# Reordering the loads, stores and modulation work of the first stage of a two-layer backbone (one core, fp32 in three products)

## The chip, the cores and the metric

The kernel runs on one core of one Trainium2 chip. The metric is the device time of one execution in microseconds (us). The kernel before takes 1304.21 us, the median of three runs (1303.91 to 1308.95). The engines are named as in the profile: PE multiplies matrices, DVE is the vector engine, ACT the scalar engine, POOL the third elementwise engine, and SP issues the DMA transfers of nearly all loads and stores. Each engine works through its own instructions in order.

## The reference, cut to what matters

Two layers act on a stream `x` of 1024 tokens with 1024 channels; 256 context tokens feed the first layer only. Each layer is modulated by a conditioning vector, and one layer's result is gated by it:

```python
shift, scale, gate = jnp.split(sc @ mod_w[l] + mod_b[l], 3, axis=-1)   # sc = silu(c); scc = silu(c_ctx) likewise
hx = modulate(rmsnorm(x, norm_g[l]), shift, scale)
hc = modulate(rmsnorm(ctx, norm_g[l]), shift_c, scale_c)               # first layer only
# first layer: va, vg, ga, xb, gb = split(h @ w_in)
#   y_a = silu(layernorm(depthwise_conv31(va * sigmoid(vg)))) * silu(ga)
#   y_b = bidirectional gated recurrence over depthwise_conv4(xb) * silu(gb); its initial states come from hc
#   out = concat(y_a, y_b) @ w_out
# second layer: u, g = split(h @ w_in); d = multi-scale pooling of u;
#   out = ((d, in 4 groups, @ w_grp) * scale * silu(g)) @ w_out
x = x + gate * out
```
The result is a final rmsnorm of `x`.

## The kernel before

**Precision.** Every fp32 operand of a large product is split in two halves, hi and lo: ACT casts the fp32 tile to hi (`wh_...`), then DVE or POOL subtracts to make lo (`wl_...`). A product is three matmuls: hi by hi, hi by lo, lo by hi. So a weight tile passes four stations before PE can use all of it: its load, the cast on ACT, the subtraction, and the PE's turn. PE can begin with hi alone; the third matmul of a triple is the first that needs lo. `wload` (L117) does load and split in one call; the engine that subtracts is an argument.

**Queues.** `load` (L107 to L115) issues a transfer on SP and ties it behind the previous one made by `load`, so that these transfers are issued in the order in which the program names them, until the first stage ends with `chain[0] = None`. SP also waits, at a transfer, for whatever the transfer needs (a store for the copy that makes its tile, a load for the last reader of its buffer), and everything behind it waits too. Elsewhere a planner orders instructions on each engine from the program's order and its own estimates of readiness.

**Folding.** The second layer's grouped product with `w_grp` is folded into a part of its input weights ahead of time (`fold`, L238 to L268). For one group, two 512 KB tiles of the group's matrix (`graw`) are loaded and split to `gh`, `gl`. Then come four steps; each loads one 512 KB weight tile `wu` and runs two sets of 12 matmuls. ACT copies each set's result to a tile `fo` (six buffers, `fpool`), and SP stores it to a DRAM buffer `wfold`, 256 KB each. The folding of two groups (16 stores) is spread over the first stage, where PE would otherwise have little to do; the buffer is read back only in the second layer, from about 795 us on. The other two groups are folded later and store from ACT's queue.

**The first stage** (L279 to L435, to about 78 us) interleaves four streams, in an order written out by hand in L396 to L435: the folding; the eight tiles of `x` (`x_load`, with squares on ACT and their sums on DVE); the first layer's modulation (`mod_loads`, `mod_cols`, in four blocks b of 512 KB x 4 loads `modw`: 16 narrow matmuls `modr` a load in groups, a copy `modrow` on ACT, then eight matmuls `modt`); and at last `modulate`, which makes the eight split tiles of the modulated stream, `h0h`, `h0l`. `rstd_cols` (L197) turns the sums of squares into the scale of each token with small matmuls (`ms_x`). At the start, before anything else on PE, two matmuls spread the conditioning vector over the partitions (`c`, L378) and ACT applies silu to it into `cL`. A short series on ACT and DVE works out the decay rates of the recurrence from `lam` (L171 to L185); it needs other ACT tables (exp) than silu.

**The context** (L383 to L394): two tiles `cx` of the context are loaded, squared, scaled by the reciprocal norm (`ctx_scale`), modulated (`modulate_ctx`) and split to `cth` (ACT) and `ctl` (DVE).

**The first products** (L672 on). PE runs `xb` (the 48 matmuls of the first recurrence input, with a small `ms_c` between them), `xbc` (24 matmuls of the same weight on the context), then the loop over eight channel blocks j: `vg` (48), `va` (48), the next block's `xbc` (24), and 12 triples of gate matmuls `g`, mixed with the next `xb`. ACT and DVE turn `xb` and `xbc` into `uc` (the short convolution), `uh` and `ul`, on which the gates depend; DVE makes `u` from `va` and the sigmoid `sg`. The weight of vg is loaded by `wload` at L678 with POOL subtracting, that of `va` by `raw_load` and `raw_split`, also with POOL. In the pass j = 0, DVE also works out the first layer's gate (L711 to L718): for each of eight blocks a 512 KB tile `modT` is loaded into a tile `L`, and one instruction multiplies it by `cL` and sums each row (a "dot" in what follows); these dots stand on DVE ahead of `u`.

After this come the conv branch's DVE work spread as "fill" steps over the loop, the output product of the first layer, and the second layer.

## Time and profile before

| | |
|---|---|
| median of 3 runs | 1304.21 us (1303.91 to 1308.95) |
| the profiled execution's own time | 1306.04 us |
| its span, first to last instruction | 1304.0 us |
| mean granted clock of PE | 0.993 |
| loaded and stored | 181.81 MB, mean 139 GB/s |

The profile comes from one execution. Its page gives busy times for each engine, and a chain of work that ended last: followed back from the last instruction, at each step to what released it. A row of the chain has the start, the length, then engine, tile and source line. A row of the timeline has start and length, engine, line, operation, the tile written and those read, partitions x elements, and in brackets how long the engine idled before and what ended that. A row of a table of windows names its columns in its head.

All that the diff touches lies in the first 120 us. There the trace shows: start to about 10 us, first loads, spreads of c, decay rates; 10 to 78 us, the first stage proper, with the DMA engines nearly full in its first two thirds; 78 to 89 us, `xb`; 89 to 98 us, part of `vg` and `xbc`; 98 to 120 us, the rest of `vg`, `va` and `xbc`, with the gate's dots on DVE; from 137 us on the loop's passes, 42.48 us each.

### The profile page before, as it was taken

The numbers are of one execution on the slowest core, as the hardware profiler recorded it, in microseconds if no ns is written. First come the engines' busy times: TensorE is split into PE (matmuls) and PEld (weight loads), VectorE is DVE, ScalarE is ACT, GpSimd is POOL, SyncE is SP. The second block draws the span as 40 slices with busy tenths as digits, with TensorE's granted clock in tenths as the row PEclk, the third lists the DMA queues.
The fourth block names the chain that finished last, engine by engine and source line by source line (L and its number), as shares of the span: only waits on it lengthen the run. The fifth ranks groups of instructions, "written<-read, shape, count | busy, mean of one in ns | idle before, by whom it ended". The sixth has DMA issues, their size and how long they took to land.

```text
span 1304.0 us, 16066 instructions
## 1 busy us (share of the span) xinstructions
PE 1267.2 (97%) x5780; PEld 1036.4 (79%) x5780; DVE 1132.8 (87%) x1756; ACT 646.1 (50%) x935; POOL 300.2 (23%) x151
## 2 busy tenths in 40 slices
PE   7999999999999999999999999999999999999995
PEld 5687888888888887888887778788888888788784
DVE  6669999999999999978968959999999987977776
ACT  7443666566566633236535346634343434645442
POOL 0212644364535546543210022000000000000002
PEclk9999999999999999999999999999999999999997
DMA  9953111122011233442418566334333334868623
GB/s 360 337 178 112 57 42 64 52 62 69 37 57 57 81 127 124 154 145 89 147 47 287 181 195 178 106 121 154 121 126 101 121 113 137 309 217 281 214 85 129
DMA packets 82865, 181.81 MB, mean 139 GB/s; under 512 B 7777, under 2 KB 27617, under 8 KB 82786
## 3 DMA queue, kind: packets, MB, share of 16 engines
q1 hardware_dynamic: 74338, 176.60, 39.9%
q10 hardware_dynamic: 8448, 4.20, 1.1%
q8 instruction: 45, 0.74, 0.2%
q14 instruction: 34, 0.28, 0.1%
HBM read 136.72 MB, written 44.04 MB: 139 GB/s over the span
## 4 chain that ended last, share of the span: by engine, by line
PE 55%; DVE 29%; DMA 8%; issue 3%; ACT 3%; POOL 1%; SPq 0%; POOLq 0%; ACTq 0%; DVEq 0%
DVE conv L444 7%; PE wob L444 6%; PE vg L444 5%; PE va L444 4%; PE xb L444 4%; DVE l L444 4%; PE g L444 3%; DMA yr_t<-y_t 2%; PE fold L262 2%; PE fold L260 2%; PE fold L261 2%; PE ga L135 2%; PE ga L444 2%; PE ga L134 2%; PE ga L136 2%
## 5 line engine op out<-in xcount | busy, mean ns | idle before, releaser
L444 DVE SCALAR_TENSOR_TENSOR conv<-u,sm,conv 128x505 f32<-128x505 f32 (+6 forms) x224 | 153.5, 745 | 1.0
L1588 POOL TENSOR_TENSOR o<-x,rr 128x256 f32<-128x256 f32 (+1 forms) x9 | 8.0, 925 | 452.6 <-ACT rr L1576 449.6
L444 ACT ACTIVATE l<-g,sm 128x512 f32<-128x512 f32 (+1 forms) x96 | 58.7, 618 | 60.0 <-PE g L444 59.2
L104 POOL TENSOR_TENSOR wl_wu<-wr_wu,wh_wu 128x1024 fp32r<-128x1024 f32 x12 | 28.7, 2390 | 171.5 <-ACT wh_wu L103 128.1
L260 PE MATMUL fold<-gh,wh_wu 128*128 128x512 f32 x128 | 53.2, 416 | 4.9 <-ACT wh_wu L103 4.9
L444 POOL TENSOR_TENSOR l<-l,l 128x1280 f32<-128x1280 f32 x16 | 47.1, 2965 | 25.6 <-ACT l L444 15.1
L444 PE MATMUL wob<-ybl,wh_wob 128*128 128x512 f32 x128 | 50.1, 392 | 2.3 <-POOL ybl L444 2.3
L261 PE MATMUL fold<-gl,wh_wu 128*128 128x512 f32 x128 | 51.7, 404 | 0.0
L262 PE MATMUL fold<-gh,wl_wu 128*128 128x512 f32 x128 | 50.3, 405 | 0.3 <-POOL wl_wu L104 0.3
L444 PE MATMUL gb<-h0h,wl_gb 128*128 128x512 f32 x128 | 49.9, 390 | 0.2 <-POOL wl_gb L444 0.2
L444 PE MATMUL gb<-h0l,wh_gb 128*128 128x512 f32 x128 | 49.8, 389 | 0.0
L444 PE MATMUL wob<-ybh,wh_wob 128*128 128x512 f32 x128 | 49.8, 389 | 0.0
L444 PE MATMUL gb<-h0h,wh_gb 128*128 128x512 f32 x128 | 49.8, 389 | 0.0
L444 PE MATMUL vg<-h0h,wh_vg 128*128 128x512 f32 x128 | 49.8, 389 | 0.0
L444 PE MATMUL vg<-h0l,wh_vg 128*128 128x512 f32 x128 | 49.8, 389 | 0.0
L444 PE MATMUL wob<-ybh,wl_wob 128*128 128x512 f32 x128 | 49.8, 389 | 0.0
L444 PE MATMUL vg<-h0h,wl_vg 128*128 128x512 f32 x128 | 49.8, 389 | 0.0
L444 PE MATMUL va<-h0h,wh_va 128*128 128x512 f32 x128 | 49.8, 389 | 0.0
L444 PE MATMUL va<-h0l,wh_va 128*128 128x512 f32 x128 | 49.8, 389 | 0.0
L444 PE MATMUL va<-h0h,wl_va 128*128 128x512 f32 x128 | 49.8, 389 | 0.0
L444 DVE TENSOR_TENSOR_SCAN l<-l,l 128x256 f32<-128x256 f32 (+1 forms) x32 | 48.7, 1521 | 1.1
L103 ACT CAST wq_g<-wr_g 128x512 fp32r<-128x512 f32 x48 | 28.2, 620 | 40.9 <-DVE wr_g L887 12.9
(593 smaller groups left out, 4291.4 us busy)
## 6 DMA issues: line engine op xcount, KB each, us to landing
wr_wu<-wu SPq DMA_DIRECT2D x16, 512.0 KB, 4.5
modw<-modW SPq DMA_DIRECT2D x16, 512.0 KB, 7.1
x_part<-xp SPq DMA_DIRECT2D x32, 256.0 KB, 2.4
mod<-modT SPq DMA_DIRECT2D x32, 256.0 KB, 3.7
wr_v<-wfold SPq DMA_DIRECT2D x16, 512.0 KB, 3.6
wr_g<-wg SPq DMA_DIRECT2D x16, 512.0 KB, 4.4
wr_wo<-wo SPq DMA_DIRECT2D x16, 512.0 KB, 4.6
yr_t<-y_t SPq DMA_DIRECT2D x16, 512.0 KB, 5.9
```

The costliest lines, as they stand in the source:

```text
L103: return (nc.scalar.copy(hi, src), eng.tensor_tensor(out=lo, in0=src, in1=hi.bitcast(F32), op=sub))
L104: eng.tensor_tensor(out=lo, in0=src, in1=hi.bitcast(F32), op=sub))
L134: nc.tensor.matmul(ps, hi[:, kc], xh[k][:, cols], start=(k == 0), stop=False)
L135: nc.tensor.matmul(ps, hi[:, kc], xl[k][:, cols], start=False, stop=False)
L136: nc.tensor.matmul(ps, lo[:, kc], xh[k][:, cols], start=False, stop=(k == ks - 1))
L260: nc.tensor.matmul(ps, wh[:, kc], gh[i], start=(i == 0), stop=False)
L261: nc.tensor.matmul(ps, wh[:, kc], gl[i], start=False, stop=False)
L262: nc.tensor.matmul(ps, wl[:, kc], gh[i], start=False, stop=(i == 3))
L444: last[eng] = f(*args, **kw)
L1588: nc.gpsimd.tensor_tensor(out=o[:, k - k0], in0=v, in1=rr, op=mult)
```

## The change

Nothing that is computed changes; where and when it is done does:

- The small tables `sm` and `eg` are loaded inside the chain, `sm` behind the second x tile and `eg` as the last of the chain. `ccol` follows `sm`, `ident` comes later. Ahead of everything now go half of group 0's matrix, the first fold weight `wu_0`, and the other half.
- The decay rates become a function that the program calls after the second block's `mod_cols`. In the planner's order its ACT instructions (Abs, exp) now stand among the squares of the first x tiles, on both sides of the silu of `cpad`.
- The stores of the first two groups' folds are collected and issued on SP behind the context's loads: six, then the load of vg's weight, then ten. The pool of `fo` tiles grows from six to eleven. In SP's order the load of va's weight stands behind the twelfth store, and the last four stores right ahead of the gate's loads.
- Ten matmuls of 128 columns on a constant tile stand at PE's start (`warm`); their result isn't used.
- The spreads of c (`spread_c`) move to before the last fold step, and use `cL` itself as the landing tile.
- The gate's loads and dots (`gates`) move from the loop's first pass to the end of the first stage, into tiles of `xpool`, as do the context's tiles `cx`. In DVE's order, dot 16 now stands behind the reciprocal of the context's norm, dot 17 between the scaling of the context and the modulation of its first half, 18 between the halves, 19 to 21 behind the second, 22 and 23 behind `ctl`.
- The weight of vg is loaded and split in the first stage, by DVE instead of POOL.
- On PE the order after `xb` becomes one matmul of `xbc`, 37 of `vg`, 23 of `xbc`, 11 of `vg`, then `va`; it was 1, 24, 23, 24. From the gate matmuls of the first pass on, the order on all engines is as before.

```diff
@@ -104,14 +104,14 @@
                 eng.tensor_tensor(out=lo, in0=src, in1=hi.bitcast(F32), op=sub))
 
 
-    chain = [None]
+    chain, chained = [None], [True]
 
     def load(out, src):
         with ExitStack() as lctx:
-            if chain[0] is not None:
+            if chained[0] and chain[0] is not None:
                 lctx.enter_context(tc.issue_after(chain[0].ins))
             d = nc.sync.dma_start(out, src)
-            if chain[0] is not None:
+            if chained[0]:
                 chain[0] = d
 
     def wload(src, name, eng, n=D, out=None):
@@ -142,9 +142,7 @@
 
 
     sm = base.tile([P, N_SM], F32, name="sm")
-    nc.sync.dma_start(sm, small)
     eg = base.tile([P, 4 * 16], F32, name="eg")
-    nc.sync.dma_start(eg, edge)
 
     def col(o, n=1):
         return sm[:, o : o + n]
@@ -168,21 +166,23 @@
     sa = base.tile([P, NL], F32, name="sa")
     sb = base.tile([P, NL], F32, name="sb")
     sz = base.tile([P, NL], F32, name="sz")
-    nc.scalar.activation(sa, lam, AF.Abs)
-    nc.scalar.activation(sa, sa, AF.Exp, scale=-1.0)
-    nc.vector.tensor_scalar(out=sb, in0=sa, scalar1=2.0, scalar2=None, op0=add)
...
-    nc.vector.tensor_scalar(out=cneg, in0=sa, scalar1=-8.0, scalar2=None, op0=mult)
+
+    def decay_rates():
+        nc.scalar.activation(sa, lam, AF.Abs)
+        nc.scalar.activation(sa, sa, AF.Exp, scale=-1.0)
+        nc.vector.tensor_scalar(out=sb, in0=sa, scalar1=2.0, scalar2=None, op0=add)
...
+        nc.vector.tensor_scalar(out=cneg, in0=sa, scalar1=-8.0, scalar2=None, op0=mult)
 
 
     def rstd(acc, eps, name, wn=0):
@@ -237,8 +237,10 @@
 
     def fold(g, raw_tile, out_tile, g_tile=None, w_tile=None):
         g_tile = g_tile or dtile
-        gh, gl = [], []
+        gh, gl, early = [], [], None
         for i in range(2):
+            if g == 0 and i == 1:
+                early = wload(wu[g, 0], f"wu_{g}_0", nc.vector)
             raw = raw_tile(f"graw_{g}_{i}")
             load(raw, grp[g, i])
             th = g_tile(f"gh_{g}_{i}", F32R)
@@ -251,8 +253,12 @@
             ws = [wload(wu[g, kp], f"wu_{g}_{kp}", nc.gpsimd, out=w_tile[kp]) for kp in range(KT // 2)]
             yield
         for kp in range(KT // 2):
-            wh, wl = (wload(wu[g, kp], f"wu_{g}_{kp}", nc.vector if g == 0 else nc.gpsimd)
-                      if w_tile is None else ws[kp])
+            if kp == 0 and early is not None:
+                wh, wl = early
+            elif w_tile is None:
+                wh, wl = wload(wu[g, kp], f"wu_{g}_{kp}", nc.vector if g == 0 else nc.gpsimd)
+            else:
+                wh, wl = ws[kp]
             for s in range(2):
                 ps = psum(f"fold_{g}_{kp}_{s}")
                 for i in range(4):
@@ -263,13 +269,22 @@
                 dst = wfold[g][:, :, 2 * kp : 2 * kp + 2, :]
                 o = out_tile(f"fo_{g}_{kp}_{s}")
                 nc.scalar.copy(o, ps)
-                (nc.sync if g < 2 else nc.scalar).dma_start(dst[:, :, s, :].rearrange("m p c -> p m c"),
-                                    o.rearrange("p (m c) -> p m c", c=P))
+                dst, o = dst[:, :, s, :].rearrange("m p c -> p m c"), o.rearrange("p (m c) -> p m c", c=P)
+                if g < 2:
+                    stores.append((dst, o))
+                else:
+                    nc.scalar.dma_start(dst, o)
             yield
 
 
     EVAC = 1000
 
+    stores = []
+
+    def store_folds(n):
+        while n and stores:
+            load(*stores.pop(0))
+            n -= 1
 
     cpool = tc.alloc_tile_pool(name="cpool", bufs=1)
     cth = [cpool.tile([P, D], F32R, name=f"cth{i}") for i in range(2)]
@@ -277,7 +292,7 @@
     cL = cpool.tile([P, D], F32, name="cL")
     hh, hl, ch, cl = [], [], [], []
     with ExitStack() as sctx:
-        fpool = sctx.enter_context(tc.tile_pool(name="fpool", bufs=6))
+        fpool = sctx.enter_context(tc.tile_pool(name="fpool", bufs=11))
         gpool = sctx.enter_context(tc.tile_pool(name="gpool", bufs=6))
         spool = sctx.enter_context(tc.tile_pool(name="spool", bufs=1))
 
@@ -293,7 +308,7 @@
             for _ in range(n):
                 next(folds, None)
 
-        cx = [spool.tile([P, D], F32, name=f"cx_{i}") for i in range(2)]
+        cx = []
 
 
         xs = []
@@ -369,16 +384,29 @@
             for h in range(2):
                 sumsq(acc[h], t[:, HALF[h]], H, k == 0, f"xsq_{k}_{h}")
 
-        chain[0] = nc.sync.dma_start(ccv, ccol)
-        nc.scalar.activation(cpad[:, :, 0:2], ccv, AF.Silu)
-        load(cx[0][:1], cc[0:1])
-        load(idx, ident)
-        ps = banks("c_0", 0)
-        for h in range(2):
-            nc.tensor.matmul(ps[h], ones[:1], cx[0][:1, HALF[h]], start=True, stop=True)
-        for h in range(2):
-            nc.scalar.activation(cL[:, HALF[h]], ps[h], AF.Silu, scale=float(D))
+        warm = psum("warm")
+        for i in range(10):
+            nc.tensor.matmul(warm[:, :P], ones, ones, start=True, stop=True)
+
+        def spread_c():
+            load(cL[:1], cc[0:1])
+            ps = banks("c_0", 0)
+            for h in range(2):
+                nc.tensor.matmul(ps[h], ones[:1], cL[:1, HALF[h]], start=True, stop=True)
+            for h in range(2):
+                nc.scalar.activation(cL[:, HALF[h]], ps[h], AF.Silu, scale=float(D))
+
+        def gates():
+            for m in range(2 * KT, 3 * KT):
+                raw = xtile(f"mod0_{m}")
+                load(raw, modT[0, m])
+                nc.vector.scalar_tensor_tensor(out=raw, in0=raw, scalar=1.0, in1=cL, op0=mult, op1=mult,
+                                               accum_out=m0[:, 0, m : m + 1])
+            nc.vector.tensor_tensor(out=m0[:, 0, 2 * KT :], in0=m0[:, 0, 2 * KT :],
+                                    in1=col(O_MB + 2 * KT, KT), op=add)
+
         def ctx_load(i):
+            cx.append(xtile(f"cx_{i}"))
             load(cx[i].rearrange("p (k n) -> p k n", n=C), ctxT[4 * i : 4 * i + 4].rearrange("k p n -> p k n"))
             for q4 in range(4):
                 sumsq(accc, cx[i][:, q4 * C : (q4 + 1) * C], C, i + q4 == 0, f"csq_{i}_{q4}")
@@ -394,22 +422,28 @@
                 modulate_ctx(k)
 
         fold_some(2)
-        for k in range(3):
+        for k in range(2):
             x_load(k)
+        load(sm, small)
+        load(ccv, ccol)
+        nc.scalar.activation(cpad[:, :, 0:2], ccv, AF.Silu)
         fold_some(1)
-        for k in range(3, 7):
+        for k in range(2, 6):
             x_load(k)
+        load(idx, ident)
         fold_some(1)
+        x_load(6)
         x_load(7)
-        mod_loads(0, range(3))
+        mod_loads(0, range(2))
         rx = [rstd_cols(acc[h][:, :H], f"x{h}", idx, spool, h) for h in range(2)]
         fold_some(1)
-        mod_loads(0, range(3, 4))
+        mod_loads(0, range(2, 4))
         mod_cols(0)
-        mod_loads(1, range(2))
+        mod_loads(1, range(1))
         fold_some(2)
-        mod_loads(1, range(2, 4))
+        mod_loads(1, range(1, 4))
         mod_cols(1)
+        decay_rates()
         modulate(0)
         modulate(1)
         mod_loads(2, range(1))
@@ -423,16 +457,23 @@
         mod_cols(3)
         modulate(4)
         modulate(5)
+        spread_c()
         fold_some(1)
         modulate(6)
         modulate(7)
         w_xb0 = wload(win[3 * KT], "xb0", nc.vector)
         ctx_load(0)
         ctx_load(1)
+        fold_some(1)
+        store_folds(6)
+        w_vg0 = wload(win[KT], "vg0", nc.vector)
         ctx_scale()
         ctx_split(0)
         ctx_split(1)
-        chain[0] = None
+        store_folds(16)
+        gates()
+        load(eg, edge)
+        chained[0] = False
 
 
     last = {}
@@ -675,7 +716,7 @@
             mm3(xb[:, HALF[h]], w, (hh, hl), HALF[h])
         xc = psum("xbc0")[:, :C]
         mm3(xc, w, (ch, cl), slice(0, C))
-        w = wload(win[KT], "vg0", nc.gpsimd)
+        w = w_vg0
         uc = utile("uc0")
         first_tap(0, xc, uc[:, :C])
         other_taps(0, xc, uc[:, :C])
@@ -708,14 +749,6 @@
             nc.sync.dma_start(raw, gw[j])
             cast(gwh, raw)
             gp(out=gwl, in0=raw, in1=gwh.bitcast(F32), op=sub)
-            if state is None:
-                for m in range(2 * KT, 3 * KT):
-                    part = L[m % 6][:, :D]
-                    nc.sync.dma_start(part, modT[0, m])
-                    vec(nc.vector.scalar_tensor_tensor, out=part, in0=part, scalar=1.0, in1=cL,
-                        op0=mult, op1=mult, accum_out=m0[:, 0, m : m + 1])
-                vec(nc.vector.tensor_tensor, out=m0[:, 0, 2 * KT :], in0=m0[:, 0, 2 * KT :],
-                    in1=col(O_MB + 2 * KT, KT), op=add)
             if state is not None:
                 rec_exp(state)
                 rec_root(state)
```

More of the change, by code (lines that the diff above doesn't have):

```diff
@@ L170, in body @@
     sz = base.tile([P, NL], F32, name="sz")
-    nc.scalar.activation(sa, lam, AF.Abs)
-    nc.scalar.activation(sa, sa, AF.Exp, scale=-1.0)
-    nc.vector.tensor_scalar(out=sb, in0=sa, scalar1=2.0, scalar2=None, op0=add)
-    nc.vector.reciprocal(sb, sb)
-    nc.vector.tensor_tensor(out=sz, in0=sa, in1=sb, op=mult)
-    nc.vector.tensor_tensor(out=sb, in0=sz, in1=sz, op=mult)
-    nc.vector.memset(sa, 1.0 / 17.0)
-    for n in range(7, -1, -1):
-        nc.vector.tensor_tensor(out=sa, in0=sa, in1=sb, op=mult)
-        nc.vector.tensor_scalar(out=sa, in0=sa, scalar1=1.0 / (2 * n + 1), scalar2=None, op0=add)
-    nc.vector.tensor_tensor(out=sa, in0=sa, in1=sz, op=mult)
-    nc.vector.tensor_scalar(out=sb, in0=lam, scalar1=-1.0, scalar2=0.0, op0=mult, op1=ALU.max)
-    nc.vector.scalar_tensor_tensor(out=sa, in0=sa, scalar=2.0, in1=sb, op0=mult, op1=add)
-    nc.vector.tensor_scalar(out=chalf, in0=sa, scalar1=4.0, scalar2=None, op0=mult)
-    nc.vector.tensor_scalar(out=cneg, in0=sa, scalar1=-8.0, scalar2=None, op0=mult)
+    def decay_rates():
+        nc.scalar.activation(sa, lam, AF.Abs)
+        nc.scalar.activation(sa, sa, AF.Exp, scale=-1.0)
+        nc.vector.tensor_scalar(out=sb, in0=sa, scalar1=2.0, scalar2=None, op0=add)
+        nc.vector.reciprocal(sb, sb)
+        nc.vector.tensor_tensor(out=sz, in0=sa, in1=sb, op=mult)
+        nc.vector.tensor_tensor(out=sb, in0=sz, in1=sz, op=mult)
+        nc.vector.memset(sa, 1.0 / 17.0)
+        for n in range(7, -1, -1):
+            nc.vector.tensor_tensor(out=sa, in0=sa, in1=sb, op=mult)
+            nc.vector.tensor_scalar(out=sa, in0=sa, scalar1=1.0 / (2 * n + 1), scalar2=None, op0=add)
+        nc.vector.tensor_tensor(out=sa, in0=sa, in1=sz, op=mult)
+        nc.vector.tensor_scalar(out=sb, in0=lam, scalar1=-1.0, scalar2=0.0, op0=mult, op1=ALU.max)
+        nc.vector.scalar_tensor_tensor(out=sa, in0=sa, scalar=2.0, in1=sb, op0=mult, op1=add)
+        nc.vector.tensor_scalar(out=chalf, in0=sa, scalar1=4.0, scalar2=None, op0=mult)
+        nc.vector.tensor_scalar(out=cneg, in0=sa, scalar1=-8.0, scalar2=None, op0=mult)
     def rstd(acc, eps, name, wn=0):
```

## The prediction

> **What bounds the kernel now.** I read the engines' busy shares first, then the windows, then the chain of work that ended last through the first 137 us, where everything that the diff touches lies, and at last the timeline at the three places where that chain is handed over.

> ```profile
> span 1304.0 us, 16066 instructions
> PE 1267.2 (97%) x5780; PEld 1036.4 (79%) x5780; DVE 1132.8 (87%) x1756; ACT 646.1 (50%) x935; POOL 300.2 (23%) x151
> PE 55%; DVE 29%; DMA 8%; issue 3%; ACT 3%; POOL 1%; SPq 0%; POOLq 0%; ACTq 0%; DVEq 0%
> ```
> PE is busy for 97% of the span and carries 55% of the chain, DVE 29%. So PE can be helped by 37 us at the very most over the whole span. Where these idle times lie decides:

> ```profile
> 10.00:20.00 10.00, 9.71 (x31) 7.71 (x32) 8.35 (x15) 8.24 (x15) 0.00 (x0) 1.00 1.03 412
> 10.00:62.00 52.00, 50.47 (x277) 36.15 (x278) 32.12 (x49) 31.58 (x47) 6.79 (x3) 0.97 0.98 370
> 62.00:78.00 16.00, 15.29 (x97) 11.50 (x98) 12.60 (x25) 10.71 (x18) 2.71 (x2) 1.00 0.77 238
> 137.00:179.50 42.50, 42.50 (x206) 35.85 (x205) 41.40 (x57) 26.47 (x30) 20.16 (x9) 1.00 0.17 56
> ```
> The columns are the window, its length, busy PE, weight load, DVE, ACT, POOL, then PE's granted clock, DMA share and GB/s. From 10 to 78 us PE idles only 1.53 + 0.71 = 2.2 us, beside DMA that is all but full until 62. In a later iteration (137 to 179.5) PE has no gap, and DVE idles 1.1 us: it waits for PE, not PE for it. Outside the first 120 us the changed kernel has the same instructions in the same order on every engine. So a shift of PE at about 122 us goes to the end as it is, and I work out that shift.

> **The start.**

> ```profile
> 3.85 5.32 DMA wr_wu<-wu
> 9.19 1.05 ACT wh_wu L103
> 10.29 0.80 PE fold L260
> 11.09 0.43 PE fold L261
> 16.68 0.23 PE fold L260
> 29.61 0.57 PE modr L326 x8
> ```
> The first weight was issued at 3.85, behind seven other loads, landed at 9.17, and after its cast the fold began at 10.29, at 0.43 us a matmul; from 16.68 on one takes 0.23. Three steps of the fold were done at 29.6.

> ```profile
> wr_wu<-wu SPq DMA_DIRECT2D x16, 512.0 KB, 4.5
> L714 SPq DMA_DIRECT2D l<-modT x8: 327/424/497, 91.5 to 111.2; - x8
> DMA to landing us min/median/max: 3.5/4.7/9.0
> 3.65 3.75 PE L378 MATMUL c<-cx,ones 1*128 1x512 f32 x4 [3.65 <-DMA cx<-cc]
> 3.93 1.28 ACT L373 ACT_TABLE_LOAD   x1
> 22.42 1.05 ACT L103 CAST wh_wu<-wr_wu 128x1024 fp32r<-128x1024 f32 x1
> L104 DVE TENSOR_TENSOR wl_wu<-wr_wu,wh_wu x4: 1219/1225/1226, 10.6 to 31.2; 128x1024 fp32r<-128x1024 f32 x4
> ```
> In the changed queue half a group matrix, the first weight, then the other half come ahead of all else. I take 3.5 us to landing for the first (the shortest of these 512 KB loads) and 512 KB at 412 GB/s, 1.27 us, between landings: 4.3, 5.6 and 6.9 us. The fold starts after the cast, at about 6.7, which is 3.6 us earlier. The ten warm-up matmuls are not in this trace. Nearest row: four records of 512 columns in 3.75 us, 0.94 each for two products. Scaled to 128 columns that is 20 records of 0.23, 4.7 us, done by 5.4, ahead of the fold. The upper end is 20 x 0.94 = 18.8 us, which holds the first step to 25 and the third to 36 (+6.4); the lower is nothing. I take nothing, since a record streams its columns. If they raise the clock, the first step (24 matmuls) takes 5.4 us at 0.227 instead of 10.3 at 0.43.

> That is not what the second step waits for. Its weight's cast stands in ACT's order behind: cast at 5.6 to 6.65, the half group from 6.9 to 7.95, squares of two x tiles (which land at 8.1 and 9.4) to 10.55, then Abs, table, silu, table, exp at 2 x 1.28 + 3 x 0.22 = 3.2 to 13.8, a fold copy of 0.59, its own 1.05: 15.45. This second table load comes from moving the decay rates. The second step runs 15.5 to 21.3. The third's cast is behind that step's second copy: 21.3 + 0.59 + 1.05 = 23.0, its low half another 1.22 on DVE; 24 matmuls end at 29.6. **Before had 29.6.** So 3.6 us earlier and a faster clock are used up by ACT's order: 0. Were the casts not in the way, the three steps would follow each other from the half group's split (6.9 + 1.05 + 1.22 = 9.2, first step's end about 12.8) and end at 12.8 + 2 x 5.45 = 23.7: -5.9, the lower end; a cold first step gives +1.5.

> From there to the first product xb, the two idle times above (2.2 us) can go, as the modulation weights no longer queue behind 12 stores, and the two spreads of c, moved in here, cost 4 records at 0.43, 1.8 us: -0.4 (bounds -2.2 and +1.8). The eight modulation loads more in the chain and the stores lie behind the loads that this stage needs.

> **The context's way.**

> ```profile
> 78.11 0.23 PE xb L134
> 82.32 1.75 DVE L194 RECIPROCAL ssqc<-sq_c 128x256 f32<-128x256 f32 x1 [2.06 <-ACT sq_c L193]
> 84.11 2.36 DVE L390 TENSOR_TENSOR cx<-cx,ssqc 128x1024 f32<-128x1024 f32 x2
> 86.39 2.67 DVE L358 TENSOR_SCALAR cx<-cx,a,m 128x256 f32<-128x256 f32 x8
> 87.80 1.05 ACT L103 CAST cth<-cx 128x1024 fp32r<-128x1024 f32 x1 [5.51 <-DVE cx L358]
> 89.47 0.12 PE xbc L134
> 79.38 0.58 ACT L265 COPY fo<-fold 128x512 f32<-128x512 f32 x1
> 117.89 1.21 DVE L444 SCALAR_TENSOR_TENSOR l<-l,cL 128x1024 f32<-128x1024 f32 x1
> ```
> Before, cth was ready at 88.85 and PE came to xbc at 89.47: 0.62 us of slack. After, DVE's order is reciprocal, dot 16, scale, dot 17, half of the modulation, and PE's order waits for the cast of that half. Two dots at 1.15 (1.21 less the overlap) add 2.3 us. Dot 16 can't start before its load lands, and **the load is behind all sixteen stores**, the last of which waits for the copy that ends at 79.96: issue of it and of the load at about 0.4 each, 80.4, plus 3.5 to 9.0 us gives 83.9 to 89.4. The reciprocal ends at 84.07. I take 4.2 us (the shortest plus one store's 256 KB, 0.65 us), 84.6: 0.5 us more. Together 2.3 + 0.5 - 0.62 = **+2.2 us** at xbc. Stage one's -0.4 only lengthens that wait. Dots 18 to 21 stand between the two modulated halves and the low parts; what PE meets ahead of the low parts is 37 vg matmuls, 8.4 us, which hide 4 x 1.15.

> **The weight of va.**

> ```profile
> 97.84 0.58 ACT uc L444
> 98.31 1.20 ACT L444 ACTIVATE uc<-xb,sm 128x1024 f32<-128x1024 f32 x1
> 99.40 1.04 ACT L444 CAST wh_va<-wr_va 128x1024 fp32r<-128x1024 f32 x1
> 100.52 2.40 POOL L444 TENSOR_TENSOR wl_va<-wr_va,wh_va 128x1024 fp32r<-128x1024 f32 x1 [18.01 <-ACT wh_va L444]
> ```
> Before, PE ran one xbc matmul, 24 of vg, 23 of xbc, 24 of vg, then va; xbc's end at 97.8 released uc on ACT, the cast of wh_va behind it, POOL's wl_va behind that, ready at 102.92. PE reached va at about 103.3. After, the order is 1, 37, 23, 11: xbc ends 13 x 0.227 = 2.95 us later against the same va. So wl_va is ready at 102.92 + 2.2 + 2.95 = 108.1, PE needs it with va's third matmul at 103.3 + 2.2 + 0.4 = 105.9: **+2.2 us**. Bounds: 0 if the cast slips ahead of uc, +2.95 if all of it shows.

> **The dots' old place.**

> ```profile
> 105.17 1.49 DVE ul L444
> 106.67 12.45 DVE l L444 x16
> 119.23 0.69 DVE u L444
> 119.97 0.96 PE g L444 x3
> PE g L444 <- DVE u L444: 1.9, 1, 1.9
> 107.73 3.41 DVE L444 SCALAR_TENSOR_TENSOR l<-l,cL 128x1024 f32<-128x1024 f32 x1
> 106.65 3.40 POOL L444 TENSOR_TENSOR wl_xb<-wr_xb,wh_xb 128x1024 fp32r<-128x1024 f32 x1 [3.73 <-ACT wh_xb L444]
> ```
> The eight dots held u to 119.23, yet PE waited only 1.9 us for it, as va and xbc filled the time. That wait goes: **-1.9**. Late next is va itself, which now ends at about 118.4 (114.0 before) and releases u. DVE thus gains 12.45 us of work at this place and only about 1 us in time.

> One dot beside POOL's split took 3.41 us instead of 1.21. [...]

> **Sum.** 0 (start), -0.4 hidden behind the context's wait, +2.2, +2.2, -1.9 = +2.5 us: span 1306.5, and with the 2.04 us around it (1306.04 for the profiled execution) 1308.5. That execution stood 1.83 us above the median of 1304.21; so I forecast 1306.7. About 0.5% (6.5 us) is what a measurement of this kernel can tell from no change.

> **Rivals.**
> A, DVE's lead is kept. DVE carries 29% of the chain, so 12.45 us taken off it could pass to the end where DVE sets the time: 1304.2 + 2.5 - 12.45 = 1294, or 1297 if a quarter is lost. Against it: u waits for va, and DVE idles 1.1 us an iteration while PE has no gap. The start's full -5.9 alone gives 1301, within my forecast's range. 0.14.
> B, the dots' loads are late (the other side). DVE works in order: reciprocal, then a dot that waits for a load behind sixteen stores; scale, modulation, cast and xbc stand behind it. With the longest landing, 9.0, it starts at 89.4 instead of 84.6: +4.8, 1311.5. If stores take twice their 0.65 us and the twelve ahead of the last four hold the load by that much, it is +7.8, 1314.5. It passes 0.5% if load 16 lands later than 88.6. For it: 16 stores and two weights lie directly ahead. Against: DMA had room by 62 to 78 us (share 0.77). 0.16.
> C, the clock falls in the two waits. PE ran at 0.43 until 16.68 and at 0.23 after; the slow stretch from 10.29 to 16.68 was 6.4 us, of which half is loss. One such stretch behind one wait gives +3.2, 1310; one behind each gives 1313. For it, the fold was slow after the 2.9 us without work from 7.40 (3.65 + 3.75) to 10.29; against it, that fold followed a stretch with hardly any work, and g followed a 1.9 us wait with 0.96 us for three matmuls, where three at 0.43 take 1.29. 0.10.
> [...]
> Forecast (1300 to 1310): 0.60.

> **Numbers.** Predicted 1306.7. Forecast and C hold 0.70, so the range reaches to B: 1298 (between the start's full gain, 1301, and A) to 1315. Faster by over 0.5%: A, 0.14. Slower: B and 0.04 of C (both stretches), 0.20. Within: 0.66.

> **What would show it.** Right: the fold's first matmul near 6.7, its third step ending near 29.6, xb near 77.7; PE waiting about 2.5 us at xbc on the cast of cth, then about 2 us in va on wl_va; no wait of g for u; iterations of 42.5 us unchanged. Wrong: the third step ending near 23.7 (the start's gain is kept); dot 16 starting after 88 (B); matmuls of 0.43 after the waits (C); the stretch from 333 us on shorter than before (A).

## The result, and the profile after

The changed kernel takes 1317.15 us, the median of six runs (1313.56 to 1320.87), beside 1305.79 us for the kernel before in its own six (1303.88 to 1308.95). The ratio is 1.0086, 95% interval 1.0063 to 1.0109: 11 us slower. The forecast was 1306.7 us, with 1315 as the top of the range.

The page of the changed kernel, profiled at 1316.59 us:

```profile
span 1314.3 us, 16075 instructions
PE 1273.6 (97%) x5800; PEld 1040.9 (79%) x5800; DVE 1129.2 (86%) x1757; ACT 648.5 (49%) x938; POOL 296.2 (23%) x150
PE 53%; DVE 27%; DMA 11%; issue 3%; ACT 3%; POOL 1%; SPq 1%; POOLq 0%; DVEq 0%; ACTq 0%
```
PE is 6.4 us busier with the same products (the 20 records of the warm-up, of 128 columns and 0.19 us each, account for 3.9 us of it; a record of 512 columns for c took 0.53), and the span is 10.3 us longer. Where the time goes is told by the start of the same work in both traces (us):

| | before | after | shift |
|---|---|---|---|
| first fold matmul | 10.29 | 6.61 | -3.7 |
| first modr, three fold steps done | 29.54 | 30.49 | +0.95 |
| first xb | 77.95 | 83.26 | +5.3 |
| first xbc | 89.30 | 97.07 | +7.8 |
| end of the first va | 114.15 | 124.47 | +10.3 |
| second vg of the loop | 136.9 | 145.0 | +8.1 |
| first qb_v after 940 us (second layer) | 952.0 | 962.3 | +10.2 |

From 138 to 941 us the shift on PE stays within 0.6 us of 8.15, as was forecast. So 8.1 us arise in the first 145 us, and two more in one place of the second layer. First the start; the chain of the changed kernel:

```profile
14.16 0.95 ACT wh_wu L103
15.14 1.24 DVE wl_wu L104
21.77 1.06 ACT wh_wu L103
22.85 1.24 DVE wl_wu L104
24.13 0.52 PE fold L268
24.64 0.43 PE fold L266
30.56 0.57 PE modr L341 x8
```
The second step waits for its cast (2.5 us), the third for its own (1.6 us), and behind these waits the third runs eight matmuls at 0.43 us. Then the windows, before (first fence) and after, from the first modr to xb:

```profile
29.54:77.94 48.40, 46.46 (x301) 32.33 (x301) 31.16 (x52) 28.50 (x40) 9.50 (x4) 0.96 0.89 311
```
```profile
30.50:83.25 52.75, 50.46 (x305) 34.00 (x304) 34.13 (x56) 30.55 (x44) 9.91 (x4) 0.94 0.76 261
```
Idle time on PE is 1.9 us before and 2.3 us after: it did not go. DMA share fell from 0.89 to 0.76, so the queue was relieved and PE did not profit. PE is busy 4.0 us longer: 2.1 us are the two spreads of c, the rest is a lower clock. The granted clock can be read from the same view (the third number from the end of a row; first fence: after, second: before):

```profile
21.07:24.48 3.41, 1.73 (x7) 0.98 (x7) 2.83 (x9) 3.19 (x6) 0.00 (x0) 1.00 1.03 411
24.48:27.89 3.41, 3.41 (x10) 2.64 (x9) 2.91 (x12) 0.43 (x1) 0.00 (x0) 0.50 1.05 417
55.20:58.61 3.41, 3.41 (x21) 1.39 (x20) 3.41 (x6) 0.76 (x1) 1.10 (x1) 0.50 0.83 274
75.68:79.09 3.41, 3.41 (x9) 2.64 (x9) 3.31 (x8) 3.40 (x9) 0.00 (x0) 0.50 1.12 346
963.15:966.56 3.41, 3.41 (x10) 2.65 (x9) 3.38 (x8) 1.14 (x2) 0.00 (x0) 0.50 0.00 0
```
```profile
29.76:33.17 3.41, 3.41 (x40) 2.21 (x32) 1.55 (x3) 2.96 (x4) 0.00 (x0) 1.00 1.06 394
33.17:36.58 3.41, 3.41 (x15) 1.75 (x15) 1.41 (x3) 0.36 (x2) 0.00 (x0) 0.50 1.08 384
```
Once the clock had first been full, the changed kernel ran at half clock in three stretches of 3.41 us ahead of xb, the kernel before in one. A fold matmul took 0.43 us in them and 0.23 outside; so, by an estimate, a stretch in which PE is always busy loses half its 3.41 us, 1.7, and the two more cost 3.4 us ahead of xb, beside 2.1 for the spreads.

What PE waits for, by the view of waits (the waiting engine, tile and line, then what ended the wait; us in all, times, longest), before in its first 140 us and, below it, after in its first 135 us:

```profile
PE modt L335 <- ACT modrow L332: 1.4, 2, 0.7
```
```profile
PE fold L266 <- ACT wh_wu L103: 5.8, 3, 2.5
PE modt L350 <- ACT modrow L347: 2.2, 3, 0.8
PE xbc L134 <- ACT cth L103: 2.2, 1, 2.2
PE va L485 <- POOL wl_va L485: 1.7, 1, 1.7
```
The chain of the changed kernel through the last fold step and the context's way (start, length, engine, tile, line):

```profile
74.92 0.51 PE fold L266
75.97 0.43 PE fold L266
78.53 0.43 PE fold L266
82.28 1.05 PE c L395 x2
87.41 0.45 PE ms_c L191 x2
88.42 1.63 issue
90.06 1.17 DVE mod L403 x2
91.22 2.28 DVE cx L418 x2
93.50 1.14 DVE mod L403 x2
94.64 1.31 DVE cx L373 x4
95.97 1.05 ACT cth L103
97.07 0.39 PE xbc L134
```
Eight matmuls of the last step run at 0.43 us (1.6 us lost), a spread of c follows on PE. Then the reciprocal (88.4, "issue"), a dot (`mod`), the scale, a second dot, the modulation, the cast, and PE at xbc: the two dots stand exactly where the prediction put them, at 1.17 and 1.14 us.

The two late microseconds lie in the second layer, in instructions that both kernels share. The first fence is the row of before's waits, the second that of after's:

```profile
PE qb_v L906 <- DVE vp L1400: 0.6, 1, 0.6
```
```profile
PE qb_v L939 <- DVE vp L1433: 2.6, 1, 2.6
```
The longer wait alone makes the two microseconds of the table. Behind it eight matmuls of qb_v run at 0.43 us, which adds 1.6 us to the shift, and 1.5 us of it are gone again at the end. In the traces of other kernels such a stretch comes at other times, from 728 us on, or not at all (before, e12, e14, e15).

### The profile page after: what moved, and what is told of

The parts are those of the page before. It is cut to its first block, busy times and chain, and to the rows that moved or that the text cites. A ratio compares the mean times of both kernels' runs of the same rounds, so it can differ in the third digit from the quotient of the medians.

```text
span 1314.3 us, 16075 instructions
## 1 busy us (share of the span) xinstructions
PE 1273.6 (97%) x5800; PEld 1040.9 (79%) x5800; DVE 1129.2 (86%) x1757; ACT 648.5 (49%) x938; POOL 296.2 (23%) x150
## 4 chain that ended last, share of the span: by engine, by line
PE 53%; DVE 27%; DMA 11%; issue 3%; ACT 3%; POOL 1%; SPq 1%; POOLq 0%; DVEq 0%; ACTq 0%
DVE conv L485 6%; PE wob L485 6%; PE va L485 5%; PE vg L485 5%; PE xb L485 4%; DVE l L485 3%; PE g L485 3%; PE ga L485 2%; PE ga L136 2%; PE ga L135 2%; PE ga L134 2%; PE xbc L485 1%; DMA wr_wu<-wu 1%; DVE u L485 1%; DMA x_part<-xp 1%
## 5 line engine op out<-in xcount | busy, mean ns | idle before, releaser
L104 POOL TENSOR_TENSOR wl_wu<-wr_wu,wh_wu 128x1024 fp32r<-128x1024 f32 x12 | 29.5, 2459 | 171.0 <-ACT wh_wu L103 171.0
L103 ACT CAST wq_g<-wr_g 128x512 fp32r<-128x512 f32 x48 | 28.1, 620 | 46.7 <-DMA wr_g<-wg 14.5
## 6 DMA issues: line engine op xcount, KB each, us to landing
wr_wu<-wu SPq DMA_DIRECT2D x16, 512.0 KB, 4.2
modw<-modW SPq DMA_DIRECT2D x16, 512.0 KB, 9.9
mod<-modT SPq DMA_DIRECT2D x16, 512.0 KB, 4.5
wr_v<-wfold SPq DMA_DIRECT2D x16, 512.0 KB, 4.3
wr_g<-wg SPq DMA_DIRECT2D x16, 512.0 KB, 4.4
wr_wo<-wo SPq DMA_DIRECT2D x16, 512.0 KB, 4.5
```

Source lines behind the costliest of these rows:

```text
L103: return (nc.scalar.copy(hi, src), eng.tensor_tensor(out=lo, in0=src, in1=hi.bitcast(F32), op=sub))
L104: eng.tensor_tensor(out=lo, in0=src, in1=hi.bitcast(F32), op=sub))
```

## The experiments

Eighteen kernels ran; "before" is the kernel before in the same runs, ratios have 95% intervals. Times in the traces are milestones as in the table above.

### One part of the change undone

**Padding in PE's gaps (e1)**, in the changed kernel:

```diff
+                pad(ps, {(0, 1, 0): 11, (0, 2, 0): 7}.get((g, kp, s), 0))   # 128-column matmuls on ones,
+                                                                          # tied behind the last fold matmul
```

> The changed kernel with 11 and 7 matmuls of 128 columns on a constant added in PE's two gaps ahead of the second and the third fold step (12.69 to 15.16 and 21.25 to 22.87 us); their result isn't used. Theory, the clock falls because of the gaps: the third step's nine matmuls at 0.43 us run at 0.23, the step ends at 28.7 instead of 30.5 us (-1.8). Rival, only the wait for the weight's cast counts and the clock falls whatever PE does in the gap: it still has matmuls of 0.43 and ends at 30.5 or, if the padding overruns the gap, later. Whole kernel: -1 to -3 us by the theory, 0 to +1 by the rival, against the changed kernel's 1317.

1318.84 us, ratio 1.0108 (1.0092 to 1.0124). The clock part came out as the theory said: no slow matmul in the third step, modr at 28.87 (-1.6), xb at 80.0 (-3.3). The gain did not reach the end: the planner, with an altered PE order, put five dots ahead of the context's cast and `ms_c` behind 30 instead of 17 matmuls of xb, and PE waited at xbc; the row of e1's waits:

```profile
PE xbc L134 <- ACT cth L103: 7.9, 1, 7.9
```

**Modulation loads split as before (e2)**: `mod_loads` with 3, 1, 2, 2 loads at the first four places.

> The changed kernel with the modulation loads split between the fold steps as before (3, 1, 2, 2 instead of 2, 2, 1, 3), so that the narrow modr matmuls of the second block lie among fold matmuls and not 24 in a row from 50.7 us. Theory, runs of narrow matmuls with a wait lower the clock: no matmuls of 0.43 between 55 and 58 us, while those at 76 to 79, behind 32 narrow ones that this edit leaves, stay; xb begins 1.7 to 2.5 us earlier than 83.3. Rival, the loss there is late loads (two loads of the third block were issued 6 us late, behind a buffer): xb begins where it did or the slow stretch stays.

1316.23 us, ratio 1.0090 (1.0074 to 1.0105). The slow matmuls between 55 and 58 us went, as the theory says, but two other stretches at half clock came (from 7.4 and 34.7 us), and xb was at 83.0, where it had been. The last step's slow matmuls stayed, as expected. So this run does not settle between the two.

**Gates back in the loop (e3)**: `gates()` taken out, the old lines of the first pass put back.

> The changed kernel with the gate's loads and dots put back into the first pass of the loop. Theory: stage one is as in the changed kernel (xb at about 83.3), the wait of xbc for cth (2.2 us) and that of va for wl_va (1.7) go, the wait of g for u (1.9) is back: -2.0 us at the gate matmuls and at the end. Rival, the dots held something that hides it (the dots' 12.45 us on DVE now show, as DVE is late anyway): the time is equal or longer, g waits 4 us or more for u.

1315.97 us, ratio 1.0075 (1.0052 to 1.0097). The wait at xbc went (11.7 us from xb to xbc instead of 13.8), and the wait of g for u was back at 1.9 us, as the theory says. The second vg began at 145.6: xb was at 84.6 in this execution, and two more slow stretches fell into it, though the order up to xb is the changed kernel's.

**The decay rates later (e4)**: `load(sm, small)` moved behind the eighth x tile.

> The changed kernel with the table sm loaded behind the eighth x tile, so that the decay rates' Abs, table load and exp leave ACT's queue ahead of the second fold weight's cast. Theory, ACT's order eats the early start: the second step starts at about 13.5 instead of 15.2 us, the third ends at 28.5 to 29 instead of 30.5, xb begins 1.5 to 3 us earlier, the same off the whole. Rival, the loads of x and of the modulation set the pace from there: the modulation's first matmuls still begin at 30.5 and xb at 83.3.

1314.71 us, ratio 1.0078 (1.0053 to 1.0103). modr at 29.4, a little short of the expectation, and xb at 81.7, which is 1.5 us earlier as expected: about a third of the stage's loss. One dot stood ahead of the cast here, and the wait at xbc was 1.2 us.

**No warm-up (e5)** and **the spreads of c at the front (e6)**, each alone in the changed kernel:

> The changed kernel without its ten warm-up matmuls. Theory, the first fold step's speed is hidden by the cast of the second weight, and a first step at 0.43 us (6.7 to 17) even leaves PE no gap ahead of the second: the modulation's first matmuls begin at 29.5 to 30.5 us as with the warm-up (30.5), xb at 82 to 83.5 (83.3). Rival, the warm-up carries the early start: they begin at 32 or later, and xb at 85 or later. (The planner also moves the context's ms_c from behind 17 to behind 30 matmuls of xb, so that the wait at xbc may grow by up to 3 us by itself.)

> The changed kernel with the spreads of c put back to the front, behind the load of ccol. Theory, they cost PE 2.1 us where the change put them, and nothing in the gap ahead of the second fold step: xb begins at about 81.2 instead of 83.3. One or two table loads more ahead of the second cast may take 1.3 us of that. Rival, another wait of the stage takes the place: xb stays at 83.

e5: 1324.91 us, ratio 1.0132 (1.0092 to 1.0172); e6: 1325.66 us, 1.0149 (1.0120 to 1.0178). Both worse than the changed kernel. Without the warm-up the third step even ended earlier (modr at 28.3): the slow first step left PE waits of only 0.5 and 0.4 us for the next two casts, and the clock did not fall behind them. So the warm-up did not carry the start; but xb was at 86.3 and 84.8, with 12 and 13 slow matmuls in the last step. In both, ACT's copy of `fo_1_1_1` moved ahead of `modrow_3`. It is the twelfth copy, and with eleven tiles it waits for the first store to land; modt waited 2.6 us behind it in e6 and 1.6 in e5. And both had five dots ahead of the cast and `ms_c` behind 30 and 34 matmuls of xb: 7.4 and 8.3 us of wait at xbc. So a single edit to this stage moves the planner's other choices by more than it is worth itself, and undoing parts in the changed kernel says little about their price. The later kernels therefore build up from the kernel before.

**Stores at once (e7)**: `load(dst, o)` in place of `stores.append((dst, o))`.

> The changed kernel with each fold store issued as soon as the program names it, in the chain, as before. Theory, the stores were not what PE waited for, and their delay gains nothing: xb at 82 to 84.5 as in the changed kernel (83.3). Rival, stores in the queue hold the modulation's loads: xb at 86 or later. At the other end of the stage, with no stores ahead of them the gate's loads land some 5 us earlier, which changes nothing, since the dots wait for the context's reciprocal there.

1406.44 us, ratio 1.0774 (1.0751 to 1.0797). This is not what the kernel before does, and my expectation missed it: there a store is free of the chain, here each is tied into it, and every load behind it waits on SP for a copy that PE has yet to feed; the row of SP's waits:

```profile
SPq L113 <- ACT fo L271: 132.9, 16, 16.9
```
Sixteen waits, 133 us of SP's time, 90 us of the kernel's. It prices a store at the wrong place of the queue, not the change's delay of them; e18 does that.

### The clock and the narrow matmuls

**Unclumped (e9)**, in the changed kernel, and **clumped (e10)**, in the kernel before:

```diff
+        mod_loads(3, range(2))          # e9
         fold_some(1)
-        mod_loads(3, range(4))
+        mod_loads(3, range(2, 4))
```
```diff
+                        if b == 3 and q == 0:          # e10
+                            mctx.enter_context(tc.issue_after(tail[0].ins))   # last matmul of the seventh fold step
                         nc.tensor.matmul(modr[b][...
```

> The changed kernel with two of the fourth modulation block's four loads named ahead of the seventh fold step, so that 12 or more fold matmuls stand between its 64 narrow matmuls and the last fold step; before the edit 32 narrow records, one spread of c and eight modt stand in a row from 70.9 to 74.9 us. Theory, a stretch of narrow matmuls lets the clock fall: the last fold step has no matmul of 0.43 us, and from the end of modt to xb it takes 6.5 to 6.8 us instead of 8.4. Rival, the clock falls at that time anyway: the slow matmuls of 76 to 79 us stay. The context's way is not judged here (the planner moves ms_c).

> The kernel before with the first narrow matmul of the fourth modulation block tied behind the last matmul of the seventh fold step, nothing else: 16 records of modr move from the middle of that step to its end, so that all stand in a row ahead of the last step. Theory, the same slow matmuls as in the changed kernel appear in the last fold step: it takes 6.8 to 7.1 us to xb instead of 5.4, and xb begins at 79.3 to 79.6 instead of 77.95; +1.5 us off the whole. Rival, order of narrow matmuls costs nothing: xb at 78, the time as before.

(A load has four narrow matmuls, eight records; the four loads of a block make 32 records.) e9: 1321.08 us, ratio 1.0122 (1.0092 to 1.0153), 13 slow matmuls in the last step. e10: 1305.06 us, 1.0003 (0.9990 to 1.0016), none. Each speaks for the rival, and the theory that such a clump always lowers the clock falls. All twenty traces together show a weaker form. In the six executions in which 3.05 us passed without a fold matmul ahead of the last step (before, e8, e12 to e15), none had a slow matmul in it. In the other fourteen that time was 3.0 (e9, 2.2 us of it idle) to 14 us, and eleven had 7 to 13 slow ones, 1.4 to 2.6 us; e1, e10 and e11 had none. e11 has the same order of PE up to there as the changed kernel, and began xb at 81.0 instead of 83.3; 1.6 us of that are the last step's.

Between the first full clock and the last 16 us of the span, every stretch at half clock in the twenty traces lasts 3.41 us or two to four times that. Two rows shown above say what came ahead of such a stretch. In the kernel before, PE was busy with narrow matmuls alone, all through 29.76 to 33.17 us, and the next 3.41 us ran at half clock. In the changed kernel the fall at 24.48 us came behind 3.41 us in which PE was busy for 1.73. Ahead of every fall in the first 150 us of the twenty traces, the full-size matmuls (128x512) filled at most 51% of the 3.41 us before it. So small a share was not always followed by a fall: in e13, behind 3.41 us with narrow matmuls alone (30.31 to 33.72 us), the clock stayed full.

### Built up from the kernel before

**Dots behind the context's split (e11)**, in the changed kernel:

```diff
+                    dctx.enter_context(tc.issue_after(parted[0].ins))     # the subtraction that makes ctl
                     nc.vector.scalar_tensor_tensor(out=raw, in0=raw, scalar=1.0, in1=cL, ...
```

> The changed kernel with the eight dots tied on DVE behind the split of the context (ctl) instead of among its steps. Theory, each dot ahead of the context's cast costs PE 1.15 us of wait: xbc begins 11.4 to 11.7 us after xb (13.8 in the changed kernel), the waits for cth and wl_va go, g does not wait for u; xb at 83.3 as there, the second vg of the loop at 141 to 142.5 instead of 145.0, the whole kernel 3 us less, 1314. Rival, the dots now hold uc on DVE and g waits for it: 144 to 146.

1310.47 us, ratio 1.0050 (1.0034 to 1.0066): 4.7 us less than the changed kernel's ratio gives. From xb to xbc 11.7 us; no wait for cth, wl_va or u; the second vg at 138.2. More than expected, as xb came 2.3 us earlier by the clock; from xb to the second vg it is 4.5 us less. Two things set the wait at xbc: the dots ahead of the cast and the place of `ms_c`. With `ms_c` behind 17 matmuls of xb it is none without a dot (e3, e11), 1.2 us with one (e4), 2.2 with two (the changed kernel). Each matmul of xb more ahead of `ms_c` adds about 0.23 us: without a dot 0.5 us behind 19 (e17, e18) and 3.0 behind 30 (e16); two dots and 23 make e2's 3.5. (e9, with one dot and 26, waits 4.6, some 1.4 more than these make.) So about 3 of the 7.4 to 8.3 us of e1, e5 and e6 are not the dots'.

**Early weight and warm-up (e8), both with dots (e12)**, in the kernel before:

```diff
+            if g == 0 and i == 1:                                         # e8, e12
+                early = wload(wu[g, 0], f"wu_{g}_0", nc.vector)
+        warm = psum("warm")                                               # e8 only
+        for i in range(10):
+            nc.tensor.matmul(warm[:, :P], ones, ones, start=True, stop=True)
+        for m in range(2 * KT, 3 * KT):                                   # e12 only, dots tied behind ctl
+            raw = xtile(f"mod0_{m}")
...
```

> The kernel before with only the first fold weight loaded between the halves of the group matrix and the ten warm-up matmuls. Theory, what the change can give is the fold's earlier start, about 1.3 us here (weight lands at 7.9, the fold begins at 9.0 instead of 10.3), and the rest of the first step's gain is lost behind the second cast: xb 0 to 2 us earlier than 77.95, the whole kernel 0 to -2 us, the same by measurement. Rival A, a full early start passes through: xb 5 us earlier, 1299. Rival B, gaps in PE lower the clock: xb later than 79.

> The kernel before with only two parts of the change: the first fold weight between the halves of the group matrix, and the gate's loads and dots at the end of the first stage, the dots tied behind the context's split. Theory: xb at 77 (-0.9), no wait of xbc, no wait of g for u (-1.9), the second vg of the loop at 134 to 134.5 instead of 136.9, the whole kernel -2 to -3 us, 1302. Rival, dots delay uc and what stands on it: no gain, 1304 to 1306; by the spread of the later waits the whole may differ by 2 us either way.

e8: 1307.64 us, ratio 1.0027 (1.0011 to 1.0042), though its xb was at 77.1 (-0.9). That is not a gain of the early weight: up to the first modr e8 is 0.3 us later (29.9), and from there to xb the trace of the kernel before has its stretch at half clock, which e8 and e12 to e15 have not (48.4 us there, 46.9 to 47.2 in these). e12: **1302.24 us, ratio 0.9979 (0.9968 to 0.9990), faster than both kernels.** Its second vg began at 132.9 (136.9 before), and the shift of -4 is still -3.7 at the end. By the rows 1.5 us of it are the half-clock stretch of the kernel before, 1.9 us the wait of g for u, which is gone. What is worth having is the move of the dots, tied behind the split; the early weight alone gains nothing (e14, below), and the tied dots without it did not run.

**Warm-up alone (e13), early weight alone (e14), e12 with warm-up (e15), e11 without (e16):**

> The kernel before with only the ten warm-up matmuls. Theory W, the warm-up changes when the clock falls later on: mean granted clock 0.990 to 0.992 over the runs instead of 0.994 to 0.995, slow matmuls in the second layer, 1306.5 to 1309 us. Rival E, the lower clock of the earlier run with weight and warm-up came from the early weight: 0.994, 1303 to 1305. Rival C, chance: no difference to the kernel before.

> The kernel before with only the first fold weight loaded between the halves of the group matrix. Theory W: mean clock 0.994 to 0.995, xb 0.9 to 1.9 us earlier than before, 1303 to 1304.5 us. Rival E: clock 0.990 to 0.992 and 1306 to 1308.

> The kernel of early weight and dots behind the context's split (1302.2 us, clock 0.995) with the ten warm-up matmuls added. Theory W: clock 0.990 to 0.992, 1304.5 to 1307 us. Rivals E and C: clock 0.995, 1301.5 to 1302.5, as the first step at full rate is hidden.

> The changed kernel with the dots behind the context's split (1310.5 us, clock 0.988 to 0.993) without the warm-up. Theory W: clock 0.993 to 0.995, 1306 to 1308.5 us. Rival, the long waits of the changed first stage lower the clock by themselves: 0.988 to 0.992, 1309 to 1313. (The planner moves ms_c from behind 17 to behind 30 matmuls of xb, with no dots in its way.)

| | us | ratio | mean clock over its runs |
|---|---|---|---|
| e13 | 1305.36 | 1.0016 (1.0002 to 1.0029) | 0.9921 (12 runs; before 0.9945, 29) |
| e14 | 1304.97 | 1.0016 (1.0004 to 1.0027) | 0.9937 (12) |
| e15 | 1302.79 | 1.0001 (0.9990 to 1.0012) | 0.9929 (12; e12: 0.9948, 12) |
| e16 | 1313.87 | 1.0083 (1.0070 to 1.0097) | 0.9898 (4; e11: 0.9899, 10) |

The warm-up costs 0.16% to 0.22% (2 to 3 us), about as theory W says, but not by its cause: it does not lower the clock later on. The mean is 0.002 lower because it counts differently. Ahead of the first grant of the full clock the profile shows 1.00: the prediction's row for 10 to 20 us says 1.00 for the kernel before, whose fold matmuls took 0.43 us until 16.68. The warm-up brings that first grant forward (at 5.0 us in e15, at 14.3 in e12), and so the half clock behind it is counted. The windows of e12, and below it those of e15:

```profile
8.40:15.23 6.83, 6.14 (x16) 4.84 (x17) 6.23 (x15) 6.07 (x9) 0.00 (x0) 1.00 1.02 414
15.30:1284.00 1268.70, 1251.92 (x5749) 1027.09 (x5747) 1108.34 (x1696) 632.27 (x914) 290.85 (x139) 1.00 0.40 136
```
```profile
8.40:15.23 6.83, 5.54 (x13) 4.38 (x14) 6.49 (x16) 6.43 (x10) 0.00 (x0) 0.50 1.03 414
15.30:1284.00 1268.70, 1252.62 (x5754) 1028.09 (x5753) 1108.48 (x1697) 632.44 (x914) 291.94 (x140) 1.00 0.41 136
```
Half of 6.83 us is 0.0026 of the span, about as much as the means differ; from 15.3 us to 1284 both ran at full clock. What e15 loses against e12 in these traces it loses at the start: the spreads of c stand behind the warm-up, both their silus then stand ahead of the weight's cast on ACT (8.59 instead of 8.00 us), and the fold begins at 9.7 instead of 9.1, modr at 29.9 instead of 29.1, the second vg at 133.8 instead of 132.9. That is 0.9 us; the rest of the 2 to 3 us stays open.

In e16 taking the warm-up away gains nothing, as the rival said: three stretches at half clock ahead of xb (e11: one), seven slow matmuls in the last fold step, and PE waited 3.0 us at xbc, with no dot but with ms_c moved back by 13 matmuls. e14 had xb at 76.5 in its trace, 1.4 us earlier than before, which is again the stretch of the kernel before (modr is at 29.6 in both); its runs are slower by 0.16%. Their mean clock is 0.0008 lower than that of the kernel before, which may be compared here, as neither has the warm-up; by an estimate that is 1 of the 2 us, and where they lie its one trace doesn't tell.

**c late (e17) and stores late (e18)**, each added to e12: the `spread_c` of the change ahead of the last fold step; `stores`, `store_folds` and eleven `fo` tiles, with the context's tiles taken from `xpool` and c loaded into `cL` as in the change.

> The kernel of early weight and dots behind the context's split (xb at 76.0, 1302.2 us) with the spreads of c moved to before the last fold step, as the change has them, and nothing else. Theory: they lie on PE's path there, two records of 0.53 us each time, xb at 78.1 (+2.1), 1304.3 us. Rival, the first of them fills the 0.7 us that PE waits for modrow: xb at 76.5 to 77.4, 1302.5 to 1303.5.

> The kernel of early weight and dots behind the context's split with the stores of the first two folds collected and issued behind the context's loads, and eleven fo tiles, as the change has it. Theory: PE did not wait for the loads that the stores held up, and what it does wait for, modrow, stays: xb at 76.0 plus or minus 0.7; the gate's loads land after 88 us and hold uc on DVE by 0 to 4 us: 1302 to 1305. Rival, the prediction's term: with no stores in the queue PE's 2.2 us of waits go, xb at 74, 1300.

e17: 1309.74 us, ratio 1.0029 (1.0012 to 1.0046), 0.50% above e12. xb was at 82.9 instead of 76.0: 6.9 us, far above both theories. Its chain and, below it, the timelines of ACT in e12 and e17 show how:

```profile
72.67 1.05 PE c L388 x2
76.39 0.43 PE fold L266
81.94 1.05 PE c L388 x2
```
```profile
22.00 1.04 ACT L103 CAST wh_wu<-wr_wu 128x1024 fp32r<-128x1024 f32 x1
22.94 0.59 ACT L271 COPY fo<-fold 128x512 f32<-128x512 f32 x1
```
```profile
23.84 0.58 ACT L271 COPY fo<-fold 128x512 f32<-128x512 f32 x1 [0.63 <-PE fold L268]
24.32 1.05 ACT L103 CAST wh_wu<-wr_wu 128x1024 fp32r<-128x1024 f32 x1
```
The spreads themselves take 2.1 us, and eight slow matmuls behind them 1.6. Of the rest, 2.3 us arise ahead of the first modr (31.45 instead of 29.11): with c gone from there, the planner puts the cast of the third step's weight behind the copy of the second step's result, so that PE waits for work that it has just finished itself (1.6 us at 23.8); in e12 the cast stands ahead of the copy. The changed kernel has that same order, with casts at 14.06 and 21.77 behind copies at 13.60 and 21.29: these are its first two waits.

e18: 1305.34 us, ratio 1.0001 (0.9986 to 1.0015), 0.22% above e12. modr at 28.8 as good as e12's 29.1, but the last step waits 0.3 us for `fo_1_1_1`, runs eight slow matmuls, and xb is at 77.7 (76.0). With no store in the queue, the two waits for modrow are 0.7 us each as before.

## Why the prediction was wrong

It was right downstream of xb and wrong upstream of it.

- **Dots, wl_va, u.** Forecast +2.2, +2.2 and -1.9. Measured: xb to xbc 13.8 instead of 11.35 us (+2.5), va's wait 1.9, and no wait of g, so that va's end to the second vg took 20.5 instead of 22.75 us (-2.2). Right in mechanism, place and nearly in size, with some luck in the first: 0.5 of its 2.2 us was a dot's load that comes late, but the load landed in time; in its place the reciprocal came 0.7 us later after xb, as `ms_c` stands behind 17 matmuls of xb and no longer behind 14. e3 and e11 show the dots as the cause: with them back in the loop, or behind the split, the waits of xbc and va are gone, and where they are tied (e11, e12) the wait of g is gone as well.
- **The start.** "0: used up by ACT's order." Fold at 6.61 (6.7 forecast), second step 15.16 (15.5), its end 21.25 (21.3). Then the third step ended at 30.5, not 29.6. The half clock behind the two waits (24.48 to 27.89 us) cost more than that; the prediction weighed it only for waits behind xb (C). e1 shows it by filling the waits: modr at 28.9, ahead of the forecast.
- **The step that failed: "the two idle times above (2.2 us) can go ... and the two spreads of c ... 1.8 us: -0.4", hidden behind the context's wait.** Measured: +4.35 from modr to xb, and +5.3 in all. Idle time stayed (2.3 us), because it is mostly PE waiting for a copy of its own result (modrow: 1.4 of 1.9 us before, 2.2 of 2.3 after) and not the queue; e18 shows that the delayed stores give nothing back. The spreads were sized nearly right (2.1 instead of 1.8). The clock had no term here at all: three half-clock stretches ahead of xb against one before, 3.4 us by the estimate above; e1, whose padded trace has none between the first step and xb, comes to xb at 80.0 instead of 83.3. Where the stretches come from is shown for the third step (the waits); for the other two, that the spreads and the longer rows of narrow matmuls bring them is argued from the counts of slow matmuls and from e17 (eight of them, 1.6 us). Moving the spreads also turns over the order of casts and copies at the front, an order that the prediction had in its sum for the start (e17: 6.9 us at xb for this part alone).
- **"Stage one's -0.4 only lengthens that wait"** assumed that the context's reciprocal stays at 82.3. It is released through ms_c, which PE runs between xb's matmuls: the context's way moves with xb, and the +5.3 went through in full.
- **A shift goes to the end as it is**: right to 941 us, then two more microseconds in this execution, as PE's wait for `vp` in the second layer was 2.6 instead of 0.6 us; why that wait grew stays open.
- **Rivals.** B had the right sign by another path: the dots' loads landed in time in the changed kernel (88.5, ahead of the reciprocal's end at 90.1); in e1, e5 and e6 the first dot, which stands ahead of the reciprocal there, began only as its load landed. C had the right mechanism at the wrong waits. A did not occur.

Built up from e12 by ratios, each to the kernel before of its own runs, the parts cost: spreads of c 0.50% (6.5 us), stores 0.22% (2.9), warm-up 0.22% (2.9), dots among the context's steps 0.36% (4.7, e11 against the changed kernel); early weight with tied dots gives -0.21% (-2.7). The sum, 14.3 us, lies above the 11 measured, but each ratio is known to 1.4 to 3 us only, so the difference says nothing.

Open: which stretches with few wide matmuls are followed by half clock and which are not, why e13 and e14 are slower by 0.16%, and what decides in which execution a wait of the second layer is followed by a slow stretch.

## What to carry to other kernels

Ask of each idle time on the bounding engine what it waits for before crediting it to a relieved queue: a wait for a copy of the engine's own last result can stay when the queue is relieved (two for modrow, 0.7 us each, with the stores in the queue and in e18 without). Where a planner orders the engines, look at every order that an edit turns over, above all casts for the next step behind copies of the last, and tie down the few instructions that must not slip ahead. Look at the stretches without wide matmuls that a small reordering lengthens: ahead of the last fold step the one of e18 (66.32 to 70.52 us, from the start of one fold matmul to that of the next) was 0.8 us longer than that of the kernel before (68.94 to 72.38), and eight matmuls at 0.43 us followed, where the kernel before had none. And before two single traces are compared, look where each had its stretches at half clock: 1.5 us of what e12 and e14 seemed to gain at xb was one stretch in the trace of the kernel before.
